# Best-entry steps, the rare group's routing and the finishes of a PEER stream at the end of a hybrid GLA / gMLP / PEER block

## The chip, the cores and the metric

The kernel runs on one core of a Trainium2 chip. The metric is device time in microseconds (us), the median of three runs. The profile is one further execution under the hardware profiler. TensorE (PE) multiplies, VectorE (DVE), ScalarE (ACT) and GpSimd (POOL) work elementwise, SyncE (SP) issues transfers; ACT and POOL issue transfers too. Each engine takes its instructions in the order of its own queue.

## The reference

One decoder block over 1024 tokens of width 1024, batch 1, float32. Only its last part is touched by the change, the PEER expert mixer: eight heads, 128 x 128 product keys, the 16 best experts per head and token.

```python
q = jnp.einsum('btd,dq->btq', h, w_q).reshape(B, T, H, 2, PEER_DQ // 2)
s1 = jnp.einsum('bthc,kc->bthk', q[..., 0, :], keys1)
s2 = jnp.einsum('bthc,kc->bthk', q[..., 1, :], keys2)
v1, i1 = lax.top_k(s1, K)
v2, i2 = lax.top_k(s2, K)
cand = v1[..., :, None] + v2[..., None, :]         # K*K candidates, indices alike
top_s, pos = lax.top_k(cand, K)
idx = jnp.take_along_axis(cidx, pos, axis=-1)
g = jax.nn.softmax(top_s, axis=-1)
...
u, vv = expert_down[ii], expert_up[ii]             # one row of 1024 each per chosen expert
a = jax.nn.gelu(jnp.einsum('pd,ped->pe', xx, u), approximate=False)
y2 = jnp.einsum('pe,ped->pd', gg * a, vv)
```

Then `x + gate2 * y2` and a final RMS norm. The inputs make the softmax so sharp that most of a head's weights fall below the smallest normal number; the kernel leaves those entries out and keeps a checked fallback (`peer_rest`) for data where its lists would not do.

## The kernel before, in words

The tokens are worked in two halves of 512 (`hf`), each of four blocks of 128 (blocks 0 to 3 and 4 to 7). Per half the weights are streamed through TensorE (three float32r products for each float32 one, L180 to L188), and at the half's end the query projection runs in five groups, with the key matmuls behind each (`s_part`, L1618). A group's scores `so` are copied to DRAM (`s_d`, L1622) and searched on VectorE for the eight best of each key half (`tops`, L199 and L200). `rank` then writes the index of each head's best entry (`dix`, L1603) and starts `route`, which computes the weights of the best entries (`dgt`, L372) and of the seven others. After the last group `pack_half` numbers the entries of the half (a count over partitions, the matmul at L312) and makes lists of them. `rare` finds the tokens and heads for which eight entries were too few (the matmul at L397, the fetch `qsc` of their scores from `s_d` at L425, and of their rows, `h2l`, at L484), searches 16 for them and packs them as a group of their own. Group 8 is that of the first half, group 9 that of the second. These are generators, stepped a piece at a time.

The experts are fetched and summed by another generator, `peer_stream`, over a list `todo` of steps (b, j):

- j below 8, a **best-entry step** (direct): the best expert of head j for each of the block's 128 tokens. GpSimd gathers 128 rows of 2048 (down and up rows, 1.05 MB, L518; `uv`, or `uvu` and `uvv` where the halves go to two buffers), VectorE takes 128 dot products (`direct_dot`, L527), ScalarE makes a diagonal matrix `Wd` of them (L532), TensorE adds `Wd` times the up rows to the block's sum `acc` (`add_rows`, L599).
- j from 8 to 16, an **entry tile**: 128 entries of the block's list. TensorE picks them from the list (`tps`, L541 and L542), ScalarE and VectorE make the index (`ix`, L550), GpSimd gathers, TensorE spreads the tokens' rows (`hps`, L571 and L572; four products), VectorE takes the dots (L573, two halves), ScalarE makes `W` (L588), TensorE sums.
- j = 17, the **row of the rare group** for a block (`rare_rows`, a matmul with `yrk`), after which the block is finished (`finish`: L695, L696, ScalarE's square L700, a power on GpSimd L168, L703, the store on SP).

The order of `todo` is group 8, blocks 0 to 3 (entry tiles and rows; their best entries are summed elsewhere), 14 best-entry steps of blocks 5, 6 and 7, six of block 4, then ten more (LATER), the last two of block 4 and its entry tiles, block 5's, group 9's six, block 6's with its row, the rows of blocks 4 and 5, block 7's tiles with its row before its last one.

What sets the order of the work: the program is written by these generators, and a scheduler then orders each engine's queue. `spare` is set within the last half's query projection; from there steps may run into the projection. `fill` issues gathers ahead of step k, up to AHD of them in the projection, into buffer pairs that RING deals out (0: a pair of `pt`, 1: two tiles of `b4`). A step from `begun + HOLD` on waits for the end of the projection (L885), where a further seven gathers ahead are allowed. From the last key matmuls on, `behind` is a hand-written order of the sums on TensorE: `queued()` puts an instruction after the last one of that list, `add_rows` adds its own to it. The count's matmul waits until the list is longer than PACK (L308). The loop at the end steps the stream and the routing in turns; until `listed` is set (at step `first + 1`, where block 4's first entry tile has the number `first`) the routing pauses once block 4 is routed, and then goes half a step (RR) for each step of the stream.

```python
            while len(use) == 1 and k >= begun + HOLD:
                yield
                nxt = fill(nxt, k)
```

Of the kernel before, what the change touches and what calls it, by code (L numbers as in the profile page):

```python
# [7 lines left out]
F32 = mybir.dt.float32  # L8
# [9 lines left out]
P = 128  # L18
D = 1024
# [11 lines left out]
NK = 128  # L31
# [15 lines left out]
WT = 4  # L47
RD = 0.62
UVC = 4
RING = (1, 0, 1, 0, 0)  # L50
RING9 = (2, 0, 1, 2, 0, 2, 1, 0, 2)
AH = 7
AHD = 4
HOLD = 8
PACK = 10
SHARE = 3
RP = .84
RP2 = .84
# [21 lines left out]
def block_kernel(ctx: ExitStack, tc: tile.TileContext, x, xT, cT, w_ada, b_ada, b_adaT, n1T, w_inp, w_alr,  # L80
# [215 lines left out]
    def pack_half(hf, tsel, rps):  # L296
        n, b0 = NCS, hf * BH
        bs = slice(b0, b0 + BH)
        g, rk = tsel[:, :, 2 * n:3 * n], tsel[:, :, 0:n]
        wk = rp.tile([P, 2, BH, n], F32, name="wk", tag="so", bufs=2)  # L300
        nz, inc = wk[:, 0], wk[:, 1]
        nc.vector.tensor_scalar(nz, g, TINY, None, op0=OP.is_ge)
        nc.vector.tensor_tensor_scan(inc.rearrange("p b n -> p (b n)"), ones[:, 0:1].to_broadcast([P, BH * n]),
                                     nz.rearrange("p b n -> p (b n)"), 0.0, op0=OP.mult, op1=OP.add)
        nc.vector.tensor_copy(e4[:, 1:], inc[:, :, n - 1])
        nc.vector.tensor_tensor(cnt[:, bs], e4[:, 1:], e4[:, :BH], op=OP.subtract)
        yield
        while hf == NHALF - 1 and len(behind) <= PACK:  # L308
            yield
        pst = rps.tile([P, BH], F32, name="aux", tag="aux")  # L310
        with queued():
            nc.tensor.matmul(pst, ltri, cnt[:, bs], start=True, stop=True)  # L312
        yield
        off = r2.tile([P, BH], F32, name="off")
        nc.vector.tensor_copy(start[:, bs], pst)
        nc.vector.tensor_tensor(off, start[:, bs], e4[:, :BH], op=OP.subtract)
        nc.vector.tensor_tensor(end[:, bs], start[:, bs], cnt[:, bs], op=OP.add)
        rki = rp.tile([P, BH, n], I32, name="rki", tag="bits")
        for i in range(BH):
            nc.vector.tensor_scalar(rki[:, i], inc[:, i], off[:, i:i + 1], None, op0=OP.add)  # L320
        nc.vector.tensor_scalar(rki, rki, P - 1, None, op0=OP.bitwise_and)
        nc.vector.scalar_tensor_tensor(rk, rki, 1.0, nz, op0=OP.add, op1=OP.mult)
        th = rp.tile([P, BH, 3 * n + 2], F32R, name="th", tag="v")
        tl = rp.tile([P, BH, 2 * n], F32R, name="tl", tag="so", bufs=2)
        nc.scalar.activation(th, tsel, AF.Identity)
        nc.vector.tensor_tensor(tl, tsel[:, :, n:3 * n], th[:, :, n:3 * n].bitcast(F32), op=OP.subtract)
        if hf == NHALF - 1:
            onchip.update({b0 + i: (th[:, i], tl[:, i]) for i in range(BH)})
        else:
            nc.scalar.dma_start(tsh_d[hf][:, :, :3 * n + 2], th.bitcast(F32))  # L330
            nc.scalar.dma_start(tsh_d[hf][:, :, 3 * n + 2:], tl.bitcast(F32))
        routed.update(range(b0, b0 + BH))
        yield
# [154 lines left out]
    def load_block(pl, b, h2):  # L488
        hh = hl = None
        if pl["own"] or b not in HRB:  # L490
            if h2 is None:
                h2 = load_h2(b)
            ph = use[turns[0] % len(use)]["ph"]
            turns[0] += 1
            hh = ph.tile([P, D], F32R, name="hh", tag="hh")
            hl = ph.tile([P, D], F32R, name="hl", tag="hl")
            nc.scalar.activation(hh, h2, AF.Identity)
            nc.vector.tensor_tensor(hl, h2, hh.bitcast(F32), op=OP.subtract)
        if b in onchip:
            return b, hh, hl, *onchip[b]  # L500
        n = ncs_of[b]
        th = pl["pw"].tile([P, 3 * NCS + 2], F32R, name="thl")[:, :3 * n + 2]
        tl = pl["pw"].tile([P, 2 * NCS], F32R, name="tll")[:, :2 * n]
        nc.scalar.dma_start(th.bitcast(F32), ts_d[b][:, :3 * n + 2])
        nc.scalar.dma_start(tl.bitcast(F32), ts_d[b][:, 3 * n + 2:])
        return b, hh, hl, th, tl

    def pair(ul, name):
        if ul is b4:
            return [b4.tile([P, D], F32, name=name + c, tag="b4") for c in "uv"]  # L510
        uv = ul.tile([P, 2 * D], F32, name=name, tag="uv")
        return [uv[:, :D], uv[:, D:], uv]

    def gather(ul, ix):
        uv = pair(ul, "uv")
        off = bass.IndirectOffsetOnAxis(ap=ix, axis=0)
        for dst, src in zip(uv, (down, up)) if ul is b4 else ((uv[2], tab),):
            nc.gpsimd.indirect_dma_start(out=dst[:], out_offset=None, in_=src, in_offset=off)  # L518
        return uv

# [248 lines left out]
    def peer_stream():  # L769
# [3 lines left out]
        def seg(b, js, open_=True, close=True):  # L773
            if open_:
                opens.add((b, js[0]))
            if js[0] < PH:
                runs.add((b, js[0]))
            todo.extend((b, j) for j in js)
            if close:
                closes.add((b, js[-1]))  # L780
# [11 lines left out]
        seg(BH, range(6, last))  # L792
        seg(BH + 1, range(PH, last))
        seg(NBLK + 1, range(PH, PH + NTR[1]))
        seg(BH + 2, rows)
        seg(BH, (last,))
        seg(BH + 1, (last,))
        seg(BH + 3, (*range(PH, last - 1), last, last - 1))
        held, turn = {}, 0
        h2s, preps, ents, es, accs, wvs = {}, {}, {}, {}, {}, {}  # L800

        def slot(k):
            if len(use) == 1:
                return (use[0]["pt"], b4)[RING[k % len(RING)] if spare else 0]
            return (use[0]["pt"], b4, use[1]["pt"])[RING9[k % len(RING9)]]

        def lists(k):
# [71 lines left out]
        yield  # L879
        first, begun = todo.index((BH, PH)), todo.index(EARLY[0][:2])  # L880
        for k, (b, j) in enumerate(todo):
            if k == first + 1:
                listed.append(True)
            nxt = fill(nxt, k)
            while len(use) == 1 and k >= begun + HOLD:  # L885
# [155 lines left out]
    with ExitStack() as pa:  # L1041
# [183 lines left out]
        for hf in range(NHALF):  # L1225
# [385 lines left out]
            def s_part(qt_of, q, i):  # L1611
                b, a0 = blks[i], 4 * q
                if q not in tvi:
                    tvi[q] = (r2.tile([P, 2 * BH, 2, KS], F32, name="tv", bufs=2),
                              r2.tile([P, 2 * BH, 2, KS], U32, name="ti", bufs=2))
                sps = auxt([P, 4, P])
                for j in range(4):
                    last_s[0:] = [nc.tensor.matmul(sps[:, j], qt_of(j), keyst[:, j % 2], start=True, stop=True).ins]  # L1618
                so = rp.tile([P, 512], F32, name="so", bufs=2)
                nc.scalar.activation(so, sps.rearrange("p a b -> p (a b)"), AF.Identity)  # L1620
                gi, bi = GRP[b]
                nc.scalar.dma_start(s_g[gi][bi][:, a0 * NK:(a0 + 4) * NK], so)  # L1622
                tops(so, i, *tvi[q])

            w_out_part(0)
# [22 lines left out]
    while qp.gens:  # L1648
        qp.pump()
        if BH not in routed:  # L1650
            qr.pump()
        elif len(rared) < 2 or listed:
            rared.append(True)
            qr.pump(RR)
    qr.drain()
    resident.clear()
    peer_rest(use[-1], Arena([use[0]["pt"].tile([P, 2 * D], F32, name="gen", tag="uv") for _ in range(3)]))
# [65 lines left out]
```

## Time and profile before

| what | value |
|---|---|
| median of 3 runs | 1483.94 us (1479.24 to 1484.35) |
| profiled execution | 1476.48 us, its span 1474.8 us |
| TensorE busy | 1362.2 us, 92% of the span |
| VectorE busy | 1092.7 us, 74% |
| ScalarE busy | 736.6 us, 50% |
| GpSimd busy | 298.2 us, 20% |
| moved by the transfers | 345.00 MB, 234 GB/s over the span |

In a row of a timeline or of groups, the operands are out<-in by the program's names, the shape is partitions by elements, x is how many instructions stand together, and the bracket has the idle time of the engine ahead of it and what ended that. In the table of stages each engine has its busy time and, in brackets, its instructions; then come the clock that TensorE was granted (1.00 is full speed), the share of time in which the transfer engines were busy, and what they moved. The rows of waits give the waiting group, what it waited for, and the total, the times and the longest.

### The profile page before, as it was taken

What the parts mean: (1) busy time and instruction counts of PE and PEld (TensorE: products, weight loads), DVE (VectorE), ACT (ScalarE), POOL (GpSimd) and SP (SyncE); (2) the same over time, 40 slices, a digit from 0 to 9 for tenths busy, and PEclk for the clock granted to TensorE, in tenths of its full rate; (3) what the DMA queues carried; (4) which work ended last, traced back from release to release, by engine and by line L of the source; (5) the groups of instructions that cost most, each with busy time, mean ns of one, the idle gap of its engine ahead of it and who ended that gap; (6) DMA issues with size and microseconds to landing.
All of it is one profiled execution on the core that took longest, in us unless ns stands there. A gap on an engine that the chain in (4) does not pass through costs nothing.

```text
span 1474.8 us, 19622 instructions
## 1 busy us (share of the span) xinstructions
PE 1362.2 (92%) x6004; PEld 1045.9 (71%) x6004; DVE 1092.7 (74%) x3114; ACT 736.6 (50%) x1611; POOL 298.2 (20%) x273
## 2 busy tenths in 40 slices
PE   3999999999998999989899999999998999789895
PEld 2778777888876977668778778877767877345452
DVE  6584768433467788898789887768899877788783
ACT  4463333333345545464535676546656555455541
POOL 0100002000000022431443133211121222552441
PEclk7899999999999999989999999999998999999998
DMA  9552644322348554675687588887688667996983
GB/s 319 182 205 93 212 146 151 102 98 98 133 156 313 185 190 164 238 267 193 205 305 235 209 300 319 305 309 258 245 317 302 239 256 252 399 408 251 370 302 128
DMA packets 120548, 345.00 MB, mean 234 GB/s; under 512 B 15001, under 2 KB 24473, under 8 KB 108146
## 3 DMA queue, kind: packets, MB, share of 16 engines
q0 software_dynamic: 31776, 165.95, 30.3%
q1 hardware_dynamic: 70416, 132.15, 26.2%
q10 hardware_dynamic: 18242, 45.58, 8.7%
q8 instruction: 48, 0.79, 0.2%
q14 instruction: 66, 0.54, 0.1%
HBM read 319.40 MB, written 24.23 MB: 233 GB/s over the span
## 4 chain that ended last, share of the span: by engine, by line
PE 67%; DVE 12%; DMA 11%; issue 4%; ACT 4%; POOL 1%; SPq 0%; ACTq 0%; DVEq 0%; POOLq 0%
PE mm L180 12%; PE mm L181 12%; PE mm L183 11%; PE acc L599 7%; PE mm L186 4%; PE mm L187 4%; PE mm L188 4%; DMA uv<-in_tab_dram,ix 3%; DMA wada<-in_w_ada_dram 2%; DMA uvd<-in_down_dram,dix 2%; PE hps L571 2%; DVE wl L1244 2%; PE hps L572 1%; PE aux L1618 1%; PE sps L1475 1%
## 5 line engine op out<-in xcount | busy, mean ns | idle before, releaser
L1243 ACT ACTIVATE wh<-wt 128x512 fp32r<-128x512 f32 x368 | 228.8, 629 | 308.8 <-PE mm L181 116.9
L1244 DVE TENSOR_TENSOR wl<-wt,wh 128x512 fp32r<-128x512 f32 x368 | 250.1, 689 | 148.6 <-ACT wh L1243 76.8
L180 PE MATMUL mm<-wh,hTh 128*128 128x512 f32 x672 | 265.3, 397 | 2.0 <-ACT wh L1243 2.0
L181 PE MATMUL mm<-wh,hTl 128*128 128x512 f32 x672 | 264.1, 395 | 0.0
L183 PE MATMUL mm<-wl,hTh 128*128 128x512 f32 x672 | 209.7, 397 | 0.0
L180 PEld LDWEIGHTS mm<-wh,hTh 128*128 128x128 f32 x672 | 127.8, 190 | 33.2 <-ACT wh L1243 3.6
L183 PEld LDWEIGHTS mm<-wl,hTh 128*128 128x128 f32 x672 | 126.7, 190 | 28.9 <-issue 1.3
L181 PEld LDWEIGHTS mm<-wh,hTl 128*128 128x128 f32 x672 | 127.5, 190 | 27.6 <-issue 0.7
L518 POOL DMA_INDIRECT uv<-in_tab_dram,ix x73 | 83.8, 1148 | 259.1 <-ACT ix L550 166.5
L186 PE MATMUL mm<-wh,hTh 128*128 128x512 f32 x224 | 90.5, 412 | 14.3 <-ACT hTh L1197 5.5
L180 PE MATMUL mm<-hTh,wh 128*128 128x512 f32 x240 | 95.4, 397 | 0.0
L181 PE MATMUL mm<-hTl,wh 128*128 128x512 f32 x240 | 94.8, 395 | 0.0
L187 PE MATMUL mm<-wl,hTh 128*128 128x512 f32 x224 | 89.9, 401 | 0.6 <-DVE wl L1244 0.6
L188 PE MATMUL mm<-wh,hTl 128*128 128x512 f32 x224 | 88.8, 399 | 0.0
L573 DVE SCALAR_TENSOR_TENSOR uv<-uv,hps 128x512 f32<-128x512 f32 x110 | 73.3, 683 | 20.2 <-DMA uv<-in_tab_dram,ix 10.4
L186 PE MATMUL mm<-hTh,wh 128*128 128x256 f32 (+1 forms) x208 | 72.5, 351 | 8.2 <-ACT vt L1288 5.6
L571 PE MATMUL hps<-hh,E 128*128 128x512 f32 x132 | 62.8, 476 | 12.6 <-DVE uv L573 10.3
L187 PE MATMUL mm<-hTl,wh 128*128 128x256 f32 (+1 forms) x208 | 70.5, 340 | 2.2 <-DVE hTl L172 2.2
L611 DVE SCALAR_TENSOR_TENSOR vl<-uv,r,vh 128x512 fp32r<-128x512 f32 x84 | 61.1, 750 | 13.6 <-PE acc L619 6.8
L183 PE MATMUL mm<-hTh,wl 128*128 128x512 f32 x240 | 70.6, 396 | 0.0
L188 PE MATMUL mm<-hTh,wl 128*128 128x256 f32 (+1 forms) x208 | 70.1, 342 | 0.3 <-DVE wl L1244 0.3
L743 POOL DMA_INDIRECT uvd<-in_down_dram,dix x32 | 39.0, 1219 | 140.6 <-DVE ts L356 46.2
(929 smaller groups left out, 2908.4 us busy)
## 6 DMA issues: line engine op xcount, KB each, us to landing
wt<-in_w_inp_dram SPq DMA_DIRECT2D x224, 256.0 KB
wt<-in_w_qp_dram SPq DMA_DIRECT2D x80, 256.0 KB
wada<-in_w_ada_dram SPq DMA_DIRECT2D x32, 512.0 KB
wt<-in_w_outp_dram SPq DMA_DIRECT2D x64, 256.0 KB
wada<-in_w_ada_dram SPq DMA_DIRECT2D x32, 256.0 KB
s_d<-so ACTq DMA_DIRECT2D x32, 256.0 KB
xr<-in_x_dram ACTq DMA_DIRECT2D x8, 512.0 KB
x_d<-x ACTq DMA_DIRECT2D x8, 512.0 KB
```

The source lines that it names most:

```text
L180: nc.tensor.matmul(ps, lh, rh, start=False, stop=False)
L181: nc.tensor.matmul(ps, *((lh, rl) if feat else (ll, rh)), start=False, stop=False)
L183: nc.tensor.matmul(ps, *((ll, rh) if feat else (lh, rl)), start=False, stop=False)
L186: nc.tensor.matmul(ps, lh, rh, start=first, stop=False)
L187: nc.tensor.matmul(ps, lh, rl, start=False, stop=False)
L188: return nc.tensor.matmul(ps, ll, rh, start=False, stop=last).ins
L518: nc.gpsimd.indirect_dma_start(out=dst[:], out_offset=None, in_=src, in_offset=off)
L571: nc.tensor.matmul(hps, Ej, hh[:, sl], start=True, stop=False)
L573: nc.vector.scalar_tensor_tensor(uv[0][:, sl], uv[0][:, sl], 1.0, hps, op0=OP.mult, op1=OP.mult, accum_out=r[:, 2 + n:3 + n])
L599: ins = nc.tensor.matmul(acc[:, sl], W, v[:, sl], start=first, stop=last).ins
L1243: nc.scalar.activation(wh, wt, AF.Identity)
L1244: nc.vector.tensor_tensor(wl, wt, wh.bitcast(F32), op=OP.subtract)
```

## The change

Constants: RING gets a sixth slot with value 2, AHD goes from 4 to 5, HOLD from 8 to 12, PACK from 10 to 9. Slot 2 is a new pair of buffers: the two tiles (`hh`, `hl`) in which the projection stage's pool keeps a block's split rows; gathers into it are made as two of 128x1024. Twelve best-entry steps (instead of eight) may now come before the hold. So that the pair is free, the split rows of block 4 come in the next stage's pool (`turns[0] + 1`).

The count's matmul is now put into `behind`. `listed` is set four steps earlier, and the routing takes a whole step where it took half of one. The end of `todo` is rearranged: block 6's tiles but for the last, block 4's row, block 6's last tile and row, three tiles of block 7, block 5's row, the rest of block 7. The four stores of the last scores to `s_d` are issued by SP instead of ACT.

```diff
-RING = (1, 0, 1, 0, 0)
+RING = (1, 0, 1, 0, 2, 0)
-AHD = 4
-HOLD = 8
-PACK = 10
+AHD = 5
+HOLD = 12
+PACK = 9
...
         with queued():
-            nc.tensor.matmul(pst, ltri, cnt[:, bs], start=True, stop=True)
+            ins = nc.tensor.matmul(pst, ltri, cnt[:, bs], start=True, stop=True).ins
+        if behind:
+            behind.append(ins)
...
-            ph = use[turns[0] % len(use)]["ph"]
+            ph = use[(turns[0] + 1) % len(use)]["ph"]
...
+    def split_pair(ul):
+        return ul is b4 or ul is use[0]["ph"]
+
     def pair(ul, name):
-        if ul is b4:
-            return [b4.tile([P, D], F32, name=name + c, tag="b4") for c in "uv"]
+        if split_pair(ul):
+            tags = ("b4", "b4") if ul is b4 else ("hh", "hl")
+            return [ul.tile([P, D], F32, name=name + c, tag=t) for c, t in zip("uv", tags)]
...
-        for dst, src in zip(uv, (down, up)) if ul is b4 else ((uv[2], tab),):
+        for dst, src in zip(uv, (down, up)) if split_pair(ul) else ((uv[2], tab),):
...
-        seg(BH + 2, rows)
+        seg(BH + 2, range(PH, last - 1), close=False)
         seg(BH, (last,))
+        seg(BH + 2, (last - 1, last), open_=False)
+        seg(BH + 3, range(PH, PH + 3), close=False)
         seg(BH + 1, (last,))
-        seg(BH + 3, (*range(PH, last - 1), last, last - 1))
+        seg(BH + 3, (*range(PH + 3, last - 1), last, last - 1), open_=False)
...
-                return (use[0]["pt"], b4)[RING[k % len(RING)] if spare else 0]
+                return (use[0]["pt"], b4, use[0]["ph"])[RING[k % len(RING)] if spare else 0]
...
-            if k == first + 1:
+            if k == first - 3:
                 listed.append(True)
...
-                nc.scalar.dma_start(s_g[gi][bi][:, a0 * NK:(a0 + 4) * NK], so)
+                eng = nc.sync if hf == NHALF - 1 and q == 3 else nc.scalar
+                eng.dma_start(s_g[gi][bi][:, a0 * NK:(a0 + 4) * NK], so)
...
-            qr.pump(RR)
+            qr.pump()
```

How the queues move, at three places. In the changed kernel the lines behind the new functions are numbered up to eight higher (L518 is L524, L599 is L605). First VectorE at the projection's end in the kernel before; `tv` and `ti` are the searches over the last scores, `hl` the second part of a block's split rows, `cand` the start of the last routing:

```order
L384 COPY tsel<-v 128x4x14
L498 TENSOR_TENSOR hl<-xr,hh 128x1024
L199 MAX tv<-so 128x8 x8
L200 MAX_INDEX ti<-tv,so 128x8 x6
...
L199 MAX tv<-so 128x8 x4
L200 MAX_INDEX ti<-tv,so 128x8 x4
L350 TENSOR_TENSOR cand<-tv 128x8x8
L350 TENSOR_TENSOR cand<-tv 128x8x4 x3
L527 SCALAR_TENSOR_TENSOR uv,rd<-uv,xr 128x1024
```

The same place in the changed kernel:

```order
L533 SCALAR_TENSOR_TENSOR uv,rd<-uv,xr 128x1024
L533 SCALAR_TENSOR_TENSOR uvu,rd<-uvu,xr 128x1024
L533 SCALAR_TENSOR_TENSOR uv,rd<-uv,xr 128x1024
L533 SCALAR_TENSOR_TENSOR uvu,rd<-uvu,xr 128x1024
L500 TENSOR_TENSOR hl<-xr,hh 128x1024
L199 MAX tv<-so 128x8 x4
...
L533 SCALAR_TENSOR_TENSOR uv,rd<-uv,xr 128x1024
L949 MEMSET more 1x1 x5
L500 TENSOR_TENSOR hl<-xr,hh 128x1024
L199 MAX tv<-so 128x8 x4
```

Four best-entry dots now stand ahead of the split rows and the searches, and a fifth with a second split stands between the searches. On TensorE, four more best-entry sums stand in the last projection group, the last of them right before the last 16 key matmuls.

Second, GpSimd's queue behind the last gathers by best entry (`dix`) in the kernel before; `ix` is an entry tile's gather, `qsc` and `h2l` the fetches of `rare`:

```order
L518 DMA uv<-in_tab_dram,dix_3_139 128x2048 x3
L518 DMA uvu<-in_down_dram,ix 128x1024
L518 DMA uvv<-in_up_dram,ix 128x1024
L518 DMA uv<-in_tab_dram,ix 128x2048 x4
L518 DMA uvu<-in_down_dram,ix 128x1024
L518 DMA uvv<-in_up_dram,ix 128x1024
L518 DMA uv<-in_tab_dram,ix 128x2048 x3
L425 DMA qsc<-s_d_109,qix 128x256
L484 DMA h2l<-h_d_107,rtok_129 128x1024
```

And in the changed kernel:

```order
L524 DMA uvv<-in_up_dram,dix_3_139 128x1024
L524 DMA uv<-in_tab_dram,dix_3_139 128x2048 x3
L427 DMA qsc<-s_d_109,qix 128x256
L486 DMA h2l<-h_d_107,rtok_129 128x1024
L524 DMA uvu<-in_down_dram,ix 128x1024
L524 DMA uvv<-in_up_dram,ix 128x1024
L524 DMA uv<-in_tab_dram,ix 128x2048 x4
```

The two fetches stood behind the gathers of nine entry tiles and now stand ahead of the first.

Third, TensorE where the rows of the rare group begin, in the kernel before (each `yrk` row ends a block):

```order
L599 MATMUL acc<-uvv,W 128x512 x2
L541 MATMUL tps<-th,E 128x170
L542 MATMUL tps<-tl,E 128x112
L599 MATMUL acc<-yrk,Wr 128x512 x2
L541 MATMUL tps<-th,E 128x170
L542 MATMUL tps<-tl,E 128x112
L599 MATMUL acc<-yrk,Wr 128x512 x2
...
L572 MATMUL hps<-hl,E 128x512
L599 MATMUL acc<-yrk,Wr 128x512 x2
```

And in the changed kernel:

```order
L605 MATMUL acc<-yrk,Wr 128x512 x2
...
L605 MATMUL acc<-uv,W 128x512 x2
L605 MATMUL acc<-yrk,Wr 128x512 x2
...
L605 MATMUL acc<-uv,W 128x512 x2
...
L605 MATMUL acc<-uvv,W 128x512 x2
...
L605 MATMUL acc<-uv,W 128x512 x2
...
L605 MATMUL acc<-yrk,Wr 128x512 x2
```

The three rows stood within one tile of each other; now one tile lies between the first and the second, and three between the second and the third.

## The prediction, on record before the run

> **What bounds the kernel now.** I read the sums by stage first, then TensorE's timeline in the stages where it is not busy, then what ended its waits, then GpSimd's and VectorE's timelines there. Busy time by stage, from the last key matmuls of the projection to the end:
>
> ```profile
> core 0: us, PE busy (x) PEld busy (x) DVE busy (x) ACT busy (x) POOL busy (x), PEclk, DMA share, GB/s
> 1195.00:1251.60 56.60, 55.92 (x259) 43.38 (x259) 44.87 (x209) 32.24 (x71) 15.43 (x15) 1.00 0.76 274
> 1251.60:1314.70 63.10, 50.22 (x124) 22.94 (x124) 52.61 (x221) 32.07 (x98) 34.87 (x30) 0.95 0.98 395
> 1314.70:1348.80 34.10, 32.42 (x107) 17.81 (x106) 28.46 (x139) 16.42 (x58) 14.24 (x16) 1.00 0.97 378
> 1348.80:1364.50 15.70, 14.50 (x49) 8.15 (x48) 13.75 (x86) 11.00 (x31) 0.04 (x1) 1.00 0.23 81
> 1364.50:1384.20 19.70, 15.65 (x52) 9.08 (x52) 14.19 (x64) 9.29 (x34) 10.47 (x11) 0.91 0.90 334
> 1384.20:1420.00 35.80, 35.48 (x118) 19.93 (x117) 26.87 (x110) 18.30 (x61) 11.67 (x13) 1.00 0.94 373
> 1420.00:1452.00 32.00, 24.99 (x76) 12.37 (x74) 22.99 (x70) 11.77 (x34) 12.49 (x11) 0.97 0.80 281
> 1452.00:1463.40 11.40, 11.32 (x24) 5.44 (x24) 4.18 (x12) 2.98 (x9) 0.00 (x0) 0.78 0.01 1
> 1463.40:1474.80 11.40, 0.00 (x0) 0.00 (x0) 4.17 (x8) 1.34 (x4) 0.54 (x1) 0.66 0.15 52
> ```
>
> Five stages matter. Up to 1251.60 (projection) TensorE is busy 55.92 of 56.60 us and the transfers have room (0.76). From there to the first entry tile at 1314.70 (the direct phase) the transfers are full (0.98) and VectorE is busy 52.61 of 63.10. Around 1348.80 to 1364.50 the transfers nearly stop (0.23), and the stage behind pays: TensorE busy 15.65 of 19.70. From 1384.20 to 1420.00 TensorE is the bound. From 1420.00 to 1452.00, where three blocks finish, it is busy 24.99 of 32.00. What TensorE waits for over all of this, and its rows at the places:
>
> ```profile
> PE acc L599 <- ACT Wd L532: 9.8, 6, 5.8
> PE hps L571 <- DVE uv L573: 9.6, 5, 3.9
> ...
> 1251.43 1.88 PE L599 MATMUL acc<-uv,Wd 128*128 128x512 f32 x4
> 1253.15 1.88 PE L599 MATMUL acc<-uvv,Wd 128*128 128x512 f32 x4
> ...
> 1273.32 8.43 PE L599 MATMUL acc<-uv,Wd 128*128 128x512 f32 x12 [5.82 <-ACT Wd L532]
> 1281.59 0.28 PE L312 MATMUL aux<-cnt,ltri 128*128 128x4 f32 x2
> 1314.71 1.88 PE L599 MATMUL acc<-uvv,W 128*128 128x512 f32 x4
> 1378.43 0.80 PE L571 MATMUL hps<-hh,E 128*128 128x512 f32 x1 [3.22 <-DVE uv L573]
> 1380.40 2.67 PE L599 MATMUL acc<-uv,W 128*128 128x512 f32 x4
> 1383.07 0.46 PE L571 MATMUL hps<-hh,E 128*128 128x512 f32 x1
> 1384.06 1.88 PE L599 MATMUL acc<-uv,W 128*128 128x512 f32 x4
> 1419.08 1.88 PE L599 MATMUL acc<-uvv,W 128*128 128x512 f32 x4
> 1420.96 1.94 PE L599 MATMUL acc<-yrk,Wr 128*128 128x512 f32 x4
> 1451.93 0.80 PE L571 MATMUL hps<-hh,E 128*128 128x512 f32 x1 [3.93 <-DVE uv L573]
> 1453.80 3.43 PE L599 MATMUL acc<-uv,W 128*128 128x512 f32 x4
> ```
>
> One step's sum costs TensorE 1.72 us (1251.43 to 1253.15). An entry tile costs 2.92: twelve of them from 1384.06 to 1419.08. Here 0.5% is 7.4 us, about what a measurement of this kernel can tell from no change.
>
> **Four more best-entry steps in the projection.** They leave the direct phase and come under the last projection group: 4 × 1.72 = 6.9 us more in a stage with 0.68 us of idle, so its end moves back by at least 6.9. Their transfers fit, GpSimd's queue shows a hole there:
>
> ```profile
> 1237.56 0.94 POOL L518 DMA_INDIRECT uvv<-in_up_dram,dix  x1 [0.61 <-DVE ts L356]
> 1252.36 0.94 POOL L518 DMA_INDIRECT uv<-in_tab_dram,dix  x1 [13.87 <-DVE ti L200]
> 1320.21 0.95 POOL L425 DMA_INDIRECT qsc<-s_d,qix  x1 [0.46 <-DVE rtok L420]
> 1347.82 0.94 POOL L518 DMA_INDIRECT uv<-in_tab_dram,ix  x1 [2.33 <-ACT ix L550]
> 1364.46 0.94 POOL L518 DMA_INDIRECT uvu<-in_down_dram,ix  x1 [15.71 <-PE acc L599]
> 1441.39 0.95 POOL L518 DMA_INDIRECT uv<-in_tab_dram,ix  x1 [0.30 <-issue]
> ```
>
> 13.87 us without an issue hold four gathers: the direct phase moved 395 GB/s × 63.1 us = 24.9 MB, and a gather is 1.05 MB, so 2.65 us each, 10.6 in all. VectorE has its dots to do there, and by the order a second split of a block's rows stands before the last top searches, behind a sum:
>
> ```profile
> L527 DVE SCALAR_TENSOR_TENSOR uv<-uv,xr 128x1024 f32<-128x1024 f32 x15 | 18.1, 1221 | 1.6 <-DMA uv<-in_tab_dram,dix 1.0 <-issue 0.5
> L527 DVE SCALAR_TENSOR_TENSOR uvu<-uvu,xr 128x1024 f32<-128x1024 f32 x4 | 4.9, 1220 | 0.0
> ...
> 1249.04 1.23 DVE L498 TENSOR_TENSOR hl<-xr,hh 128x1024 fp32r<-128x1024 f32 x1 [2.68 <-ACT hh L497]
> ```
>
> Queued behind those five dots and that split are the searches over the last scores, and behind them the last routing. VectorE is idle 11.7 us of this stage (56.60 − 44.87), which takes four dots of 1.22 and a split of 1.23 (6.1 us). I add 1.1 for the places where it doesn't fit: the end of the projection moves by **+8.0**, with 6.9 as the low end and 12 (6.9 plus the two splits' 1.23 and 2.68 of waiting) as the high one.
>
> The direct phase gets shorter. Its transfers: five gathers fewer are left to issue after the projection's end (19 to 14), so 24.9 − 5.2 = 19.7 MB, at 395 GB/s 49.9 us. VectorE: 52.61 − 4 × 1.22 = 47.7, plus some 1.5 of the rare group's work that now comes into it, 49.2. Neither runs without gaps: before, VectorE's 52.61 took 63.10, an excess of 10.5, of which 5.82 is one stop of TensorE. I keep a bit under half of the excess: 54, **−9.1**, with ends 50 (transfers alone) and 62. Net of the two: −1.1 (from −6 to +11). The sixth pair is what lets five gathers run ahead; every split pair issues twice, and every second slot is split instead of two in five, two more issues over twenty steps, 2 × 1.24 us on a GpSimd that is busy 34.87 of 63.10: nothing, hidden under the transfers. The Trainium skill ("DMA: Bandwidth & Descriptors", Anatomy of one DMA) fits a GpSimd transfer at 2.0 us plus its bytes; paid one behind the other, two more would make this phase some 4 us longer, estimated from that page. The trace doesn't bear it out here: whole and halved gathers together kept the queues at 0.98.
>
> The count's matmul is made part of TensorE's hand-written order, nine sums after the key matmuls instead of ten; what is queued behind it are all later sums. At 1281.59 it waited for nothing; its operand is due 1.72 us earlier and one dot's load on VectorE less. 0, with 5.8 (the longest wait of the phase) as the high end.
>
> **Rare group's routing from the packing on, without half steps.** Before, its scores were fetched at 1320.21, between entry gathers, and the lists of its own tiles came so late that GpSimd issued no gather for 15.71 us after 1347.82, up to 1364.46. By the order, the fetch now stands ahead of the first entry gather, nine gathers earlier. At 2.92 us per tile its pack should be there some 26 us earlier, against a hole of 15.71: the hole goes. What it cost is not 15.71: buffers were full when it began, and TensorE stood 3.22 us at 1378.43 plus 0.83 in the smaller waits before it (19.70 − 15.65 = 4.05 idle). Behind the stop the clock was 0.91 and the matmuls were slow: the sum at 1380.40 took 2.67 for 1.88, the four products before it 1.97 (1378.43 to 1380.40) for 0.99 (1383.07 to 1384.06), together some 1.8. So **−5.8**, with 0 as the other end. The Trainium skill ("TensorE: Matmul & The Clock Gate", HAM oscillation) has the clock fall after idle stretches of over some 3.4 us; by that a wait of 3.22 costs only itself, and this term would be −4.0. The row shows the slow matmuls, so I keep the 1.8. What is late next is the transfers, which must then carry 1.05 MB in 2.92 us (359 GB/s); they did 373 from 1384.20 on.
>
> The same routing has VectorE at 13.75 of 15.70 between 1348.80 and 1364.50. Spread over more tiles its share per tile falls; TensorE's idle there is 1.2 and in the stage before 1.7. **−1.0**, ends −2.9 and +1.
>
> **Finishes spread.** Three blocks' last rows came together from 1420.96 on, in this order 6, 4, 5, and their finishing passes stood on VectorE at once:
>
> ```profile
> L695 DVE TENSOR_TENSOR yr<-acc,g2row 128x1024 f32<-128x1024 f32 x3 | 3.7, 1223 | 0.0
> L696 DVE TENSOR_TENSOR yr<-yr 128x1024 f32<-128x1024 f32 x3 | 3.7, 1221 | 0.0
> L703 DVE SCALAR_TENSOR_TENSOR yr<-yr,fs,fw 128x1024 f32<-128x1024 f32 x2 | 2.6, 1277 | 0.0
> ...
> 1451.17 0.69 DVE L573 SCALAR_TENSOR_TENSOR uv<-uv,hps 128x512 f32<-128x512 f32 x1 [6.31 <-DMA uv<-in_tab_dram,ix]
> ```
>
> With one more L703 that is 11.3 us of VectorE, ahead of dots that TensorE and the gathers wait for (the buffers come free late, so the last gather goes out at 1441.39, and VectorE stands 6.31 us for a landing). From 1420.96 to 1463.40 are 42.4 us, for nine tiles of 2.92 and four row sums of 1.72: 33.2. The excess is 9.2: 7.0 of idle up to 1452.00 and the slow matmuls after the stop of 3.93 (the sum at 1453.80 took 3.43). Now block 4's rows come before the last tile of block 6, block 6's after it, and block 5's three tiles later. The passes are the same, no tile waits for two of them at once. I take **−7.0**, ends −9.2 and 0: the last block's gathers still end the kernel, and their last landing keeps some of it. The end behind the last sum, 11.40 us, stays.
>
> **Four stores of the last scores on SyncE.** They leave ScalarE's queue; on SyncE only the output stores are behind them. 0.
>
> **Sum.** −1.1 − 5.8 − 1.0 − 7.0 = −14.9. Against the profiled execution, 1476.5 (its span of 1474.8 and 1.7 around it): 1461.6. The three timed runs lie above it, their median 7.5 higher at 1483.94; by it I forecast **1469.0**.
>
> **The rivals.**
> *More in the direct phase.* If it runs at the transfers' 50 us and the finishes lose their whole 9.2: −21, 1463; with the projection moved by 6.9 only, 1462. For it: 13.87 us of hole in the queue just before. Against: VectorE's 49.2 stands as close.
> *Only the later terms, or half of all.* If VectorE holds the direct phase at 61 (its dots and the rare group's lists now compete), the first term is +5.9, and with half of the finishes (−3.5) the sum is −4.4: 1479.5, no change that can be told. For it: VectorE in order, 0.83 busy in this phase, and its work moves into it, not out.
> *Slower, by VectorE's order at the projection's end.* The second split waits for the sum of the first of the four added steps, since it takes over that step's buffer. Behind it are the last searches, the last key matmuls and the routing. In the loaded queues a gather took 9.8 us from its issue (1441.39) to its dot (1451.17). If two of the four steps pay issue to landing, dot and sum one behind the other, 2 × (9.8 + 1.22 + 1.72) = 25.5, the projection ends 26.7 later with the split; with −9.1 and the other terms' −13.8 that is +3.8, and two stops like that at 1451.93 bring slow matmuls of some 2.4 each (1453.80's 3.43 for 1.88, and 1.87 for 0.99 in the products before it): +8.6, 1492.5. It decides from a delay of 23 us on. Against: the hole of 13.87 us holds those gathers.
> *The change doesn't do what it says:* the hole in GpSimd's queue could stay, if the rare group's lists wait for their pack as before: −9.1, 1474.8.
>
> **How the numbers follow.** Forecast 0.47 (1464 to 1476); more 0.20; half 0.18; not as said 0.05; slower 0.10. Faster by over 0.5% (under 1476.5) are the forecast, more, and 0.03 of not as said: 0.70. Within 0.5% (up to 1491.4) are half and the rest of not as said: 0.20. Slower: 0.10. The range leaves out the slower case. Its lower end takes all the low ends, 6.9 − 13.1 − 5.8 − 2.9 − 9.2 = −24.1, and 2 us for the spread of the timed runs: 1458. Its upper end is half, 1479.5, and 3.5 more for finishes that bring nothing: 1483.
>
> **What would show it.** In the changed profile: the last key matmuls some 8 us later and the first entry sum about 54 us behind them; the fetch of the rare group's scores ahead of the first entry gather and no hole of over 5 us among the gathers after it; no stop of TensorE over 2 us between the first entry tile and the last; from the first row sum of a second-half block to the last sum some 35 us. Wrong would be: a projection that ends over 12 us later, a direct phase over 60 us, or the same stop before the rare group's tiles.

## The result, and the profile after

The changed kernel takes 1468.3 us (median of 20 runs) where the kernel before takes 1480.0 (20 runs): a ratio of 0.993, interval 0.9911 to 0.9949, or 10.4 us less by the ratio (11.7 by the medians). Two later sets of runs, each on one chip, gave 0.9933 (0.9909 to 0.9958) and 0.9931 (0.9907 to 0.9954). The forecast was 14.9 us less, 1469.0, with a range of 1458 to 1483. That 1469.0 and 1468.3 lie so close is in part luck: the three runs that the forecast started from had a median of 1483.94, 3.9 above that of the 20, and the gain was put 3 to 4.5 us too high, so the two errors cancel.

Two single profiles can't be set side by side by their clocks: at a matmul that both kernels reach with the same order on TensorE (the last one that waits for `hTl` ahead of the first query group), they stood at 1116.44 and 1113.79, and over all the executions below this place moved between 1111 and 1128, whatever the kernel. So all stages are counted from that matmul, called the common matmul below. The table of stages of the changed kernel, from there to the end of the key matmuls (projection), to the first entry sum (direct phase), to the 22nd entry sum, to the first row of the rare group in the second half's blocks, to the last sum, and the end:

```profile
core 0: us, PE busy (x) PEld busy (x) DVE busy (x) ACT busy (x) POOL busy (x), PEclk, DMA share, GB/s
1113.79:1263.49 149.70, 143.05 (x722) 114.36 (x723) 115.83 (x441) 79.16 (x172) 41.03 (x36) 0.97 0.76 269
1263.49:1318.07 54.58, 44.45 (x110) 20.38 (x109) 49.53 (x216) 28.72 (x83) 24.92 (x23) 0.91 0.95 366
1318.07:1384.27 66.20, 63.16 (x212) 35.61 (x212) 57.80 (x288) 38.42 (x130) 27.84 (x29) 1.00 0.92 361
1384.27:1416.73 32.46, 31.71 (x103) 17.57 (x103) 24.10 (x96) 16.15 (x53) 8.97 (x9) 1.00 0.92 341
1416.73:1451.42 34.69, 32.49 (x101) 17.12 (x100) 27.79 (x83) 14.84 (x45) 9.80 (x11) 1.00 0.67 256
1451.42:1464.70 13.28, 1.88 (x5) 0.57 (x3) 4.22 (x8) 1.33 (x4) 0.55 (x1) 0.72 0.13 46
```

And the first of these stages in the kernel before:

```profile
1116.44:1251.60 135.16, 134.00 (x706) 110.79 (x707) 111.34 (x430) 76.30 (x160) 27.61 (x27) 0.98 0.73 262
```

The projection got 14.5 us longer: it holds 16 more matmuls (the four sums), but TensorE is also idle 6.65 us where it was idle 1.16. The direct phase is 54.6 long, for 63.1. From the first to the last entry sum it is 133.4 (66.20 + 32.46 + 34.69), for 146.7. What TensorE waited for in that last part of the changed kernel, with total, times and the longest wait:

```profile
PE acc L605 <- ACT W L594: 4.0, 7, 1.5
PE acc L605 <- issue: 1.1, 3, 0.5
PE hps L577 <- DVE uv L579: 0.6, 2, 0.3
```

Before, the wait for VectorE's dots alone was 9.6 us over five times. GpSimd's queue of the changed kernel, with the fetch of the rare group's scores, the first entry gather, and the longest stretch without an issue behind it:

```profile
1293.51 0.95 POOL L427 DMA_INDIRECT qsc<-s_d,qix  x1 [1.37 <-DVE rtok L422]
...
1304.30 1.48 POOL L524 DMA_INDIRECT uvu<-in_down_dram,ix  x1 [8.59 <-issue]
...
1336.58 0.98 POOL L524 DMA_INDIRECT uvu<-in_down_dram,ix  x1 [9.96 <-ACT r L589]
```

The fetch came ahead of the first entry gather, as the order said. A stretch of 9.96 us without an issue is still there, only earlier, and TensorE has no wait of over 0.5 us in the 40 us behind it.

### The profile page after: what moved, and what is told of

The parts are those of the page before. It is cut to its first block, busy times and chain, and to the rows that moved or that the text cites. A ratio compares the mean times of both kernels' runs of the same rounds, so it can differ in the third digit from the quotient of the medians.

```text
span 1464.7 us, 19631 instructions
## 1 busy us (share of the span) xinstructions
PE 1354.2 (92%) x6004; PEld 1040.5 (71%) x6004; DVE 1092.9 (75%) x3114; ACT 735.9 (50%) x1611; POOL 297.5 (20%) x275
## 4 chain that ended last, share of the span: by engine, by line
PE 61%; DVE 15%; DMA 12%; issue 6%; ACT 4%; POOL 1%; ACTq 0%; SPq 0%; DVEq 0%; another core or an unknown queue 0%; POOLq 0%
PE mm L180 10%; PE mm L181 10%; PE mm L183 10%; PE acc L605 6%; PE mm L186 4%; PE mm L187 4%; PE mm L188 4%; DMA uvd<-in_down_dram,dix 2%; DMA wada<-in_w_ada_dram 2%; DMA uv<-in_tab_dram,ix 2%; DVE wl L1252 2%; DVE uv L579 1%; PE hps L577 1%; DMA uv<-in_tab_dram,dix 1%; DMA wt<-in_w_qp_dram 1%
## 5 line engine op out<-in xcount | busy, mean ns | idle before, releaser
L524 POOL DMA_INDIRECT uv<-in_tab_dram,ix x74 | 84.5, 1142 | 265.9 <-ACT ix L556 158.7
L186 PE MATMUL mm<-wh,hTh 128*128 128x512 f32 x224 | 91.1, 413 | 14.9 <-ACT hTh L1205 5.9
L579 DVE SCALAR_TENSOR_TENSOR uv<-uv,hps 128x512 f32<-128x512 f32 x112 | 74.8, 682 | 13.5 <-PE hps L578 5.0
L617 DVE SCALAR_TENSOR_TENSOR vl<-uv,r,vh 128x512 fp32r<-128x512 f32 x84 | 61.0, 748 | 13.8 <-PE acc L625 5.7
```

The source lines that it names most:

```text
L186: nc.tensor.matmul(ps, lh, rh, start=first, stop=False)
L579: nc.vector.scalar_tensor_tensor(uv[0][:, sl], uv[0][:, sl], 1.0, hps, op0=OP.mult, op1=OP.mult, accum_out=r[:, 2 + n:3 + n])
```

## The experiments

Each variant's sum is over the three stages: projection, direct phase, first to last entry sum (sums are of the unrounded times). Each row is one profile; the ratio is that of the timed runs.

| kernel | projection | direct | entries | sum | ratio to before |
|---|---|---|---|---|---|
| before | 135.2 | 63.1 | 146.7 | 345.0 | 1 |
| before_again | 135.4 | 65.2 | 146.1 | 346.6 | 1 |
| changed | 149.7 | 54.6 | 133.4 | 337.6 | 0.993 |
| changed_again | 152.3 | 54.4 | 133.3 | 340.0 | 0.9933 |
| changed_third | 147.7 | 54.1 | 133.4 | 335.2 | 0.9931 |
| projection_part_alone | 149.8 | 51.7 | 150.9 | 352.4 | 1.004 |
| no_projection_part | 135.7 | 64.7 | 131.4 | 331.9 | 0.9948 * |
| no_projection_part_2 | 136.7 | 66.7 | 132.2 | 335.5 | 0.9898 |
| hold_8_only | 142.5 | 61.7 | 133.3 | 337.5 | 0.9935 |
| old_ring_hold_12 | 140.8 | 56.0 | 134.0 | 330.8 | 0.9888 |
| finishes_together | 148.5 | 54.1 | 141.4 | 344.0 | 1.0051 * |
| routing_half_steps | 150.8 | 53.5 | 134.1 | 338.4 | 0.9992 * |
| count_free | 151.9 | 56.3 | 132.4 | 340.5 | 1.0001 * |
| count_free_2 | 153.1 | 57.5 | 134.1 | 344.7 | 0.9928 |

The four ratios with a star come from one chip, on which the kernel before ran at 1471.8 us; on the others it ran at 1477.7 to 1480.3. Two of the four variants were run again on another chip and came out 0.0050 and 0.0073 lower. Their own medians hardly moved (1463.5 and 1466.1, 1471.7 and 1470.3), so it is the kernel before that was faster there. An estimate from these two is that the other two read some 0.006 too high as well; the changed kernel itself was not run on that chip. Why the kernel before was better there was not found; no profile of it was taken there. By the means of the profiles the sum fell by 8.2 us, for the 10.4 of the timed runs; three profiles of the changed kernel alone lie between 335.2 and 340.0.

**The changed kernel and the kernel before, again**, with no edit.

> The changed kernel itself, beside the variants below on one chip, since the four variants before were set against the kernel before at 1471.8 and the changed kernel at 1480.0. Theory D (the change is worth the same there): ratio 0.993, and then the parts taken out before cost 0.012 (finishes), 0.006 (half steps), 0.007 (count) and give 0.002 (projection part). Theory E (where the kernel before runs at 1472 its tail has smaller stops, and the change is worth less): 0.997 to 0.998, and the parts are worth some 7 us less each, the projection part costs 3 to 5.

Theory D held for the changed kernel's ratio on the chip it got; the prices that D puts on the parts fell, by the repeats below.

> The kernel before, for a second profile of it. Theory D: from the matmul behind the last hTl wait to the key matmuls' end 135 us, direct phase 63, first entry sum to the last 147, as in the first profile. Theory E: the same order but shorter stops, the last part 140 or less.

D: 135.4, 65.2 and 146.1.

> The changed kernel a third time, as the measure for the three beside it on the same chip: 0.993. If this chip's kernel before lies near 1472 and the ratio is 0.997 or 0.998, then the first four variants were set against a better kernel before, and their distances to the changed kernel are some 0.004 smaller than they look.

0.9931, with the kernel before at 1480.3. So the chip of the starred ratios was the odd one.

**The projection part alone**, on the kernel before:

```diff
-RING = (1, 0, 1, 0, 0)
+RING = (1, 0, 1, 0, 2, 0)
...
-AHD = 4
-HOLD = 8
+AHD = 5
+HOLD = 12
...
-            ph = use[turns[0] % len(use)]["ph"]
+            ph = use[(turns[0] + 1) % len(use)]["ph"]
...
```

With it come `split_pair` and the third choice in `slot`, as in the change.

> The kernel before with HOLD 12, AHD 5, the sixth slot of RING and the place of block 4's split rows; nothing else. Theory A (the part costs what the traces add up to, 14.6 - 8.5): some 6 us slower than before, 1.004. Theory B (as predicted, -1.1): 0.999. Rival (more, the later stages catch what the projection loses, since their waits were for transfers that are now earlier): 0.996 or less.

1.004 (1.0022 to 1.0059): 5.9 us slower, theory A. Its stages:

```profile
1114.14:1263.96 149.82, 144.18 (x722) 115.30 (x723) 117.31 (x451) 79.20 (x172) 43.83 (x36) 0.97 0.76 274
1263.96:1315.67 51.71, 42.50 (x109) 18.75 (x107) 45.19 (x192) 28.00 (x83) 22.01 (x21) 0.97 0.85 326
1315.67:1466.52 150.85, 134.42 (x413) 73.15 (x414) 111.47 (x480) 69.56 (x230) 53.10 (x53) 0.95 0.81 309
```

14.5 to 14.7 more in the projection, 11.4 to 13.5 less in the direct phase, and 4 to 5 more behind it (against the two profiles of the kernel before).

**The changed kernel without that part**, the same edit the other way; run twice.

> The changed kernel with HOLD, AHD, RING and the place of block 4's split rows as before; the rest of the change stays. Theory A (the parts add up, and by the two traces the projection part costs more than it gives: projection 14.6 us longer from a common matmul, direct phase 8.5 us shorter): this is some 6 us faster than the changed kernel, a ratio to the kernel before of 0.989; first entry sum about 63 us behind the last key matmuls, about 133 us from the first entry sum to the last. Theory B (the part pays for itself, as its term of -1.1 us said): 0.994. Theory C (the early routing only works because the direct phase got shorter; with ten more steps behind the projection the routing crowds it): 0.997 or more, with the direct phase over 66 us.

> The changed kernel without HOLD 12, AHD 5, the sixth slot and block 4's new place, again. Theory A (the projection part costs what it cost alone, 5.9 us): 0.989, some 6 us below the changed kernel of the same call. Theory F (it costs alone, but nothing in the whole, since the routing's whole steps need the time that the longer projection gives): within 2 us of the changed kernel.

0.9898 (0.9867 to 0.9930), beside 0.9931 on the same chip: 5 us below the changed kernel by the medians, 1466.1 and 1471.1. This speaks for theory A; the intervals overlap, so F (no price in the whole) is not excluded by the times alone. C falls: no ratio of 0.997 or more; of the direct phases, 64.7 and 66.7, one is over C's 66, but the kernel before has 63.1 and 65.2.

**HOLD 8 only**, the sixth pair and the rest stay:

```diff
-HOLD = 12
+HOLD = 8
```

> The changed kernel with HOLD 8 only; the sixth pair, five gathers ahead and all else stay. Theory A (what costs in the projection are the four sums, 6.9 us, and their stops): the key matmuls end some 7 us earlier, the direct phase is some 7 us longer, the total within 3 us of the changed kernel. Rival (the loss of some 5 us early in the projection, with TensorE's wait of 2.7 us for the query's eviction, comes from the sixth pair's place in the order and not from the four steps): that wait stays with HOLD 8 as well.

The stages up to the first entry sum, and the longest wait of TensorE in the projection:

```profile
1116.69:1259.17 142.48, 136.04 (x706) 111.78 (x707) 111.39 (x429) 76.90 (x162) 35.86 (x30) 0.97 0.73 261
1259.17:1320.89 61.72, 49.16 (x125) 22.88 (x124) 55.59 (x248) 32.06 (x98) 35.42 (x31) 0.92 0.97 387
```

```profile
PE tps L1525 <- ACT qt L1594: 3.1, 1, 3.1
```

Both statements held. The total is that of the changed kernel (0.9935): against its first profile, the four steps cost the projection 7 us and give the direct phase 7. And the rival: with the same 706 matmuls as in the kernel before, the projection is still 7.3 longer. TensorE is idle 6.44 us there where it was idle 1.16, with the wait for the query's eviction (the copy of its products out of TensorE's result memory by ScalarE, `qt`); the other 2 us are slower matmuls. That loss comes with the sixth pair.

**The old ring with HOLD 12**, five pairs and five gathers ahead:

```diff
-RING = (1, 0, 1, 0, 2, 0)
+RING = (1, 0, 1, 0, 0)
-            ph = use[(turns[0] + 1) % len(use)]["ph"]
+            ph = use[turns[0] % len(use)]["ph"]
```

> The changed kernel with HOLD 12 and AHD 5, but the old RING of five pairs and block 4's split rows at the old place. Theory G (the sixth pair, by its place in the order, costs the projection 6.8 us, the wait of 2.7 to 3.5 us for the query's eviction among them, and gives the direct phase 3.0): that wait is gone, the projection part from the common matmul on takes 143 us for 150, the direct phase 55 to 58, and the kernel is some 4 us faster than the changed one: 0.990. Rival (without the sixth pair the four steps' gathers come late in the projection, and TensorE or the last searches wait for them): the projection part 150 us or more, 0.995 or above.

```profile
1119.48:1260.31 140.83, 140.18 (x722) 113.14 (x723) 116.54 (x442) 79.41 (x172) 34.10 (x33) 0.98 0.76 270
1260.31:1316.30 55.99, 44.03 (x108) 20.22 (x108) 47.24 (x225) 28.37 (x83) 25.26 (x23) 0.88 0.96 363
1316.30:1450.32 134.02, 127.39 (x415) 70.43 (x414) 109.67 (x458) 69.06 (x229) 49.72 (x50) 1.00 0.87 333
```

Theory G: 0.9888 (0.9857 to 0.9919), 1465.5 us from six runs, the lowest ratio of all, 15 us below the kernel before and 5.6 below the changed one on the same chip (the intervals of these two overlap, so that it beats the changed kernel is likely and not shown). The same 722 matmuls as in the changed kernel, and 0.65 us of idle instead of 6.65. Five pairs were enough for the twelve steps and for five gathers ahead: the direct phase is 56.0. The sixth pair and the new place of block 4's split rows, which it needs, were taken out together; this run doesn't part them.

**The finishes together**, the old end of the list in the changed kernel:

```diff
-        seg(BH + 2, range(PH, last - 1), close=False)
+        seg(BH + 2, rows)
         seg(BH, (last,))
-        seg(BH + 2, (last - 1, last), open_=False)
-        seg(BH + 3, range(PH, PH + 3), close=False)
         seg(BH + 1, (last,))
-        seg(BH + 3, (*range(PH + 3, last - 1), last, last - 1), open_=False)
+        seg(BH + 3, (*range(PH, last - 1), last, last - 1))
```

> The changed kernel with the old order of todo at the end (rows of blocks 6, 4 and 5 together). Theory A (the spread is worth its term, measured 7.2 us between the two traces): ratio to the kernel before 0.998, VectorE's L695, L696 and L703 again close together and stops of TensorE of over 3 us there. Rival (the stop before the last tiles came from gathers that were late since the rare group's hole, which is gone either way): 0.993 to 0.995, with no stop over 2 us.

TensorE's waits from the first to the last entry sum, and the rows ahead of the last tiles:

```profile
PE hps L577 <- DVE uv L579: 7.5, 5, 5.3
```

```profile
1456.29 0.79 PE L577 MATMUL hps<-hh,E 128*128 128x512 f32 x1 [5.26 <-DVE uv L579]
...
1459.32 3.50 PE L605 MATMUL acc<-uv,W 128*128 128x512 f32 x4
```

The stop is back, 5.26 us with the hole of 15.7 us gone, and with it the slow sum behind it, 3.50: theory A, and the rival falls. The entries take 141.4 for 133.4: 8.0 us. The ratio, 1.0051, would say 0.012 (18 us); less the 0.006 by which that chip's ratios are estimated to read too high it is 9 us.

**Half steps of the routing**, in the changed kernel:

```diff
-            if k == first - 3:
+            if k == first + 1:
...
-            qr.pump()
+            qr.pump(RR)
```

> The changed kernel with listed set at first + 1 and half steps of the routing as before. Theory A (this is what fills the hole in GpSimd's queue, worth 6.1 us): ratio 0.997, a hole of 10 us or more ahead of the rare group's gathers. Rival (the hole is filled already because the count comes earlier and is pinned, and the fetch needs few steps): 0.993.

GpSimd's queue, and the stages of the hole, behind it and after that:

```profile
1347.88 0.94 POOL L524 DMA_INDIRECT uv<-in_tab_dram,ix  x1 [2.33 <-ACT ix L556]
1364.50 0.94 POOL L524 DMA_INDIRECT uvu<-in_down_dram,ix  x1 [15.68 <-PE acc L605]
```

```profile
1348.80:1364.50 15.70, 14.50 (x49) 8.14 (x49) 13.78 (x86) 10.98 (x31) 0.02 (x2) 1.00 0.45 187
1364.50:1384.20 19.70, 18.52 (x66) 10.53 (x65) 17.95 (x82) 11.21 (x42) 13.37 (x14) 1.00 0.91 339
1384.20:1420.00 35.80, 34.88 (x115) 19.53 (x114) 26.58 (x99) 17.41 (x60) 10.30 (x10) 1.00 1.01 409
```

A result that neither side expected. The hole is back, to the tenth (15.68 us), as theory A said, and it costs next to nothing: the entries take 134.1 for 133.4, and the ratio, less 0.006, is that of the changed kernel. TensorE is idle 1.2 us in the stage behind the hole, where the kernel before was idle 4.05. During the hole 187 GB/s were still coming in, where it was 81, and later on the transfers went at 409 GB/s. The stock of gathered tiles is not what differs: when the hole began, 18 entry gathers had been issued and 11 tiles summed, in this kernel as in both profiles of the kernel before and in the projection part alone, and TensorE's order behind the hole is that of the kernel before. What differs is when the first tile gathered behind the hole was summed: 7.3 us after the hole's end here, 8.6 and 9.3 in the kernel before, 12.7 in the projection part alone. Why is open, and this is one profile.

**The count free**, run twice:

```diff
-PACK = 9
+PACK = 10
...
-            ins = nc.tensor.matmul(pst, ltri, cnt[:, bs], start=True, stop=True).ins
-        if behind:
-            behind.append(ins)
+            nc.tensor.matmul(pst, ltri, cnt[:, bs], start=True, stop=True)
```

> The changed kernel with PACK 10 and the count's matmul not in the hand-written order. Theory A (it costs and gives nothing): ratio 0.993 and the same direct phase of 55 us within 2. Rival (the pinned count is what brings the packing early enough; free, it slides behind more sums): the direct phase 3 us longer, 0.995.

> The changed kernel with PACK 10 and a free count, again. Theory A (nothing): within 2 us of the changed kernel of the same call, as the profiles from the common matmul on say (340.5 against 337.6 and 340.0). Rival (it is worth 0.007, as the ratios across two chips say): 8 to 10 us above the changed kernel.

0.9928 beside 0.9931 on the same chip: nothing, theory A. The direct phase is some 2 to 3 us longer in both profiles (56.3 and 57.5), as the rival of the first expectation said, but the totals don't show it. Of the rearrangement, the stores on SyncE were not tried by themselves.

## Why the prediction was right, and where it was off

- **The end of the projection, +8.0: mis-sized.** Measured +12.4 to +17.0 in the three profiles of the changed kernel (against 135.3, the mean of the two before), +14.5 in the first: outside the ends of 6.9 and 12, and one of the prediction's own signs of being wrong ("a projection that ends over 12 us later"). The four sums were priced well: the old ring with HOLD 12 has the projection 5.6 us longer (140.8 for 135.2) and no more idle time than before. The step that failed is "two more issues over twenty steps [...] nothing, hidden under the transfers", the sixth pair's. It was priced by GpSimd's issue time in the direct phase alone. Its cost is in the projection, 6.9 to 11.4 us against the old ring with HOLD 12; in the first profile 5.5 us more idle than before and some 2 of slow matmuls. In the changed kernel, the gathers of the first two best-entry steps (the first in two issues, of which one is shown), VectorE's dot of the second, ScalarE's step on it, and the next key matmuls:

```profile
1169.09 0.94 POOL L524 DMA_INDIRECT uvu<-in_down_dram,dix  x1 [23.84 <-DVE cidx L352]
...
1172.86 3.89 POOL L524 DMA_INDIRECT uv<-in_tab_dram,dix  x1 [0.30 <-issue]
...
1182.10 1.23 DVE L533 SCALAR_TENSOR_TENSOR uv<-uv,xr 128x1024 f32<-128x1024 f32 x1 [3.98 <-DMA uv<-in_tab_dram,dix]
1183.36 0.20 ACT L535 ACTIVATE rd<-rd 128x1 f32<-128x1 f32 x1 [5.28 <-DVE uv L533]
1184.62 0.71 PE L1626 MATMUL aux<-keyst,qt 128*128 128x128 f32 x4 [1.30 <-ACT qt L1578]
```

  The same gathers and the dot of the second in the kernel before:

```profile
1168.83 0.94 POOL L518 DMA_INDIRECT uv<-in_tab_dram,dix  x1 [24.43 <-DVE ts L356]
1170.07 0.95 POOL L518 DMA_INDIRECT uvu<-in_down_dram,dix  x1 [0.30 <-DMA wt<-in_w_qp_dram]
...
1177.46 1.22 DVE L527 SCALAR_TENSOR_TENSOR uvu<-uvu,xr 128x1024 f32<-128x1024 f32 x1 [0.80 <-DMA uvu<-in_down_dram,dix]
```

  RING deals out slots by the step's number modulo its length, so a sixth slot changes which steps are split. Before, the first best-entry gather was a whole one and the second a split one, of which the dot needs the down rows alone. Now the first is split and the second whole. The dot waits for the landing and starts 68.3 us behind the common matmul, where it was 61.0; ScalarE's step on it (`rd`) stands ahead of the query's evictions in its queue, and the key matmuls wait for these. That wait, 1.3 to 1.5 us, is in all nine profiles with the sixth pair and in none of the five without it. A second wait comes earlier and is longer, but not in every execution:

```profile
1133.95 0.63 ACT L1251 ACTIVATE wh<-wt 128x512 fp32r<-128x512 f32 x1 [2.87 <-DMA wt<-in_w_qp_dram]
...
1135.30 1.09 PE L1525 MATMUL tps<-ident,xr 128*128 128x128 f32 x8 [2.70 <-ACT qt L1594]
...
1137.64 0.63 PE L578 MATMUL hps<-hl,E 128*128 128x512 f32 x1
```

  Here the eviction stood behind the copy of a weight tile (`wh`) that came late; behind the wait a matmul of 512 columns took 0.63 us for 0.39. The wait was 2.7, 3.5 and none in the three profiles of the changed kernel, 1.0 to 3.6 in the others with the sixth pair, and at most 0.8 without it. VectorE's order differs from 2.4 us behind the common matmul on, TensorE's from 36 us on, well ahead of the last key matmuls; the prediction read the orders only where the change's own instructions stand. What makes the weights late in most executions and not in all was not found.
- **The direct phase, −9.1 to 54: right.** 54.6, 54.4 and 54.1, with the kernel before at 63.1 and 65.2. Its parts were right too: VectorE was busy 49.5 us (49.2 was said), and 366 GB/s over 54.6 us are 20.0 MB (19.7). Only that the sixth pair is what lets five gathers run ahead was wrong: five pairs did it in 56.0.
- **The net of the two, −1.1: wrong in sign.** 14.5 − 8.5 = +6.0 by the two first profiles; +5.9 for the part alone by its ratio, and about +5 in the whole (there the intervals overlap).
- **The count, 0: right** beside the routing's whole steps; with half steps it was not tried. The stores, 0: not tested.
- **The rare group's hole, −5.8, and its work, −1.0, and the finishes, −7.0: right in size, but what brought the first two is open.** Together −13.8; measured −13.0 (146.4, the mean of the two profiles before, to 133.4), and −14.2 to −15.0 in the two profiles without the projection part. The 25th entry sum is block 6's first; all kernels reach it ahead of the finishes, and cut there the stage falls into two parts:

| kernel | GpSimd's hole | finishes | first to 25th entry sum | 25th to last |
|---|---|---|---|---|
| before, before_again | 15.7 | together | 82.3, 81.5 | 64.4, 64.6 |
| projection_part_alone | 15.7 | together | 86.9 | 64.0 |
| finishes_together | 10.0 | together | 76.0 | 65.4 |
| routing_half_steps | 15.7 | spread | 77.5 | 56.6 |
| changed, three profiles | 9.9 to 10.0 | spread | 76.2 to 76.3 | 57.1 |
| no_projection_part, two | 9.4 | spread | 74.4, 75.1 | 57.0 |

  The last column goes by the finishes alone, whatever the hole: 64.0 to 65.4 in the four profiles with them together, 56.6 to 57.5 in all ten with them spread. Their term is shown, 7.4 us for the 7.0 forecast. The column before it fell by 5.6 us in the changed kernel and by 7.1 without the projection part, for the 6.8 forecast, but what brought it is not shown. With the routing's half steps the hole is back and the time is not; freeing the count and taking out the projection part don't bring it back either. Ahead of the 25th sum, the kernel with half steps (77.5) and the projection part alone (86.9) were written differently only in the count's place and the queue of the stores; neither was taken back together with the routing.
- **The end behind the last sum, and the stretch from the first row of blocks 4 to 7 to the last sum, 35 us:** 34.7, and 11.40 behind the last sum, as said. TensorE's longest wait between the first entry tile and the last was 1.5 us, under the 2 that were said. Of the other signs, "no hole of over 5 us" was wrong (9.96), and it didn't matter.
- **The rivals.** None took over: 10.4 to 11.7 us less lies nearer to the forecast's 14.9 than to the 4.4 of "half" or the 21 of "more". The mechanism that the slower one named is there, but small: at the projection's end late dots hold ScalarE's eviction of the last scores, and TensorE waits for it 1.4, 2.2 and 2.3 us in the three profiles, where it was 0.7 and 0.5. Most of the loss in the projection lies ahead of that.
- **The rule on the clock.** I kept 1.8 us of slow matmuls behind the stop of 3.22. The second profile of the kernel before has them behind a shorter stop, a sum of 3.35 us after a wait of 1.76, with a granted clock of 0.67 from 1378 to 1382:

```profile
1376.79 3.35 PE L599 MATMUL acc<-uvv,W 128*128 128x512 f32 x4 [1.76 <-issue]
```

  The trace doesn't agree with the Trainium skill ("TensorE: Matmul & The Clock Gate", HAM oscillation), which has the clock fall after idle gaps of over some 3.4 us: here 1.76, 2.70 and 3.22 were each followed by slow matmuls.

## What to carry to other kernels

A buffer added to a ring is not only issue time and space: it changes which step gets which kind of buffer, and with that when its data land and what stands behind them in another engine's queue. So read the orders of all engines from their first difference on, not only where the edit's instructions stand. A hole in a queue has no price by its length: the same 15.7 us, with the same stock of tiles, cost from next to nothing to some 10 us in four profiles. Cut a stage at a piece of work that all kernels reach alike, and count from one: up to the common matmul single executions differed by more than the change gave, and cut at the 25th sum, the share of the finishes stood apart from the rest.

## What the runs showed of the hardware

The time up to the common matmul, which all kernels reach with the same order on TensorE, moved between 1111 and 1128 us from one execution to the next, 17 us, more than the whole change gives. On one chip the kernel before took 1471.8 us (35 runs) where on others it took 1477.7 to 1480.3, and two variants of the changed kernel, at nearly the same time on both chips, gained 0.005 and 0.007 less there; the cause is open.
